# First output projection of a two-layer encoder: seven block products in place of eight, prepared during the attention heads

## The chip, the cores and the metric

One core of one Trainium2 chip runs the whole program. The metric is the device time of one execution in microseconds (us), the median of several runs. The core has five engines with a queue each: PE (TensorE, matrix products into PSUM banks), DVE (VectorE), ACT (ScalarE), POOL (GpSimd) and SP (SyncE, which here issues all the transfers). Each queue runs in its program order; engines wait for one another through semaphores, and while an instruction waits, everything behind it on its engine waits too.

## The reference

The program is an encoder trunk of two layers over 1024 tokens of width 1024, in fp32. Layer 0 is differential attention with 8 heads, layer 1 is latent attention. Cut to what the change touches:

```python
shift, scale, gate = _modulation(c, ada_w[i], ada_b[i])
h = _rmsnorm(x, norm_g[i]) * (1.0 + scale) + shift
# layer 0, _diff_attention:
o = _rmsnorm(o, subln_g) * (1.0 - lambda_init)
o = o.reshape(b, s, DA_WIDTH) * jax.nn.silu(z)
y = o @ w_out                 # (1024, 1024) by (1024, 1024)
...
x = x + gate * y              # gate: one number per output column
```

The change is in `o @ w_out` of layer 0, in where `gate` is applied, and in how `o` and `w_out` come to that product.

## The kernel before

**Products.** An fp32 operand is held as two rounded parts, a high and a low one, and each 128x128 by 128x512 product is three matmuls into one PSUM bank: high by high, high by low, low by high (`mm3`, L186 to L188). To split a 128x512 tile, ACT casts it (the high part) and POOL or DVE subtracts (the low part). In tile names, `wh`, `woh`, `oah`, `oth` are high parts, and `wl`, `wol`, `oal`, `otl` low ones.

**Stages.** From the start of the span: norm, modulation, V and the first K and Q up to about 170 us; heads 0 to 6 of layer 0 up to about 632 us; head 7 up to about 692 us; the first output projection up to 779 us; then layer 1, whose own output projection, at the end of the span, is already made of seven block products (class `Seven`, lines 1827 to 1890 or so).

**A head** (`attn0`) has eight slots: four query tiles by the two halves of differential attention. In a slot PE makes scores, transposes the probabilities and multiplies by V; between these, `FILL0` puts steps of the next head's projections on PE (`acc<-h0h,wh` and so on), whose weights ACT and POOL split (`wl`, L232). At the end of half a head its output goes through the head norm: ACT squares (`osq`), PE sums, POOL does the last step of the reciprocal root (`rq_y`, L173 and L946) and multiplies the output by it (L886) and by the SiLU gate (L931). Hooks run these steps one slot after the other. The last hook (`split`, L889) splits the output on ACT (L894) and POOL (L895) and stores both parts to DRAM (`oS`, L896 and L897).

**The gate.** `gate_steps0` runs one step a slot through heads 0 to 6: loads of the modulation weights and dot products on DVE, five slots for each of eight, then a store to `gateS`.

**Head 7** has no next head to project. From slot 2 on (`Z_LAST`), `extra0` loads outputs and weights of the projection (`pre_plan`), and `PRE0` says how many steps of the projection PE makes in each slot: 12 steps of three matmuls, the heads 0 to 5 of two tiles of 128 tokens (`Pre.step`). `run_tails` ends the head with the calls 8 to 10 of `extra0`.

**The projection** (`out_proj`, L1139) computes four quarters: two groups of 512 tokens by two halves of 512 columns. In a quarter, 8 heads by 4 token tiles make 96 matmuls into four banks named `oacc`; that is 384 in all, 36 of them in head 7. The weights are loaded (`wor`) and split by ACT (L1115) and POOL (L1116, `wol`). The result is multiplied by the broadcast gate on DVE (L1167, `oy<-oacc,gb`, one PSUM and one SBUF input) and added to x (L1168, two SBUF inputs). When a group is complete, its norm runs (`group0`), and steps of the next stage are given out one by one (`side.tick`). The second half of head 7 is finished between the first matmuls of the projection (`tail0`): L933, the sums, `rq_y`, L910, PE's broadcast `rb` (L911), L912, and a split by ACT and DVE (L917).

**Order.** While the table `mk` is filled, POOL's instructions stay in program order (`in_turn`), and ACT's casts and some of DVE's are kept behind the marked ones (`behind`). Elsewhere a scheduler orders each queue when the program is built.

Of the kernel before, what the change touches and what calls it, by code (L numbers as in the profile page):

```python
# [48 lines left out]
PRE0 = (0, 0, 0, 0, 2, 1, 2, 2, 2, 2, 1)  # L49
PRE_N = 6  # L50
PRE1 = (0, 0, 0, 0, 0, 0, 0, 1, 1, 1, 1)
OW0 = (3, 4)
OP0 = (6, 4)
# [31 lines left out]
def trunk(ctx: ExitStack, tc: tile.TileContext, A, out):  # L85
# [49 lines left out]
    oS = dr.tile([NH, 2, 2, P, HF], F32, name="oS")  # L135
    oF = dr.tile([NH, 2, P, HF], F32, name="oF")
    tS = dr.tile([7, 4, P, HF], F32, name="tS")
    sS = dr.tile([4, 2, P, HF], F32, name="sS")
# [741 lines left out]
    def finish(o, y, l, h, half, dst, ap_, dgs):  # L880

        if dst is None:
            b, rb = bcast_rows(ap_, y, "osq", 4)

            def scale():
                in_turn(G.tensor_mul(t3(o), t3(o), rb))  # L886
                hooks.append(split)

            def split():  # L889
                if l == 1:  # L890
                    SP.dma_start(oF[h, half], o)
                    return
                with behind("S"):
                    S.copy(b.bitcast(F32R), o)  # L894
                in_turn(G.tensor_sub(o.bitcast(F32R), o, b))  # L895
# [8 lines left out]
        rb = bank("z" if l else "m", "rb")  # L904
# [8 lines left out]
        if l == 1:  # L913
            return
        hi, lo = dst
        S.copy(hi, o)
        V.tensor_sub(lo, o, f32v(hi))  # L917
# [9 lines left out]
    def subln(o, sq, zz, half, h, dst):  # L927
# [7 lines left out]
        def rest():  # L935
            pt = ssq_at[0] if dst is None and ssq_at else bank("acc" if dst is None else "tr", "ssq")
# [10 lines left out]
            finish(o, y, 0, h, half, dst, a0b if dst is None else None, sq)  # L947

        if dst is None and h < NH - 1:
            hooks.append(rest)  # L950
        else:
            rest()
# [109 lines left out]
    def gate_steps0():  # L1062
# [4 lines left out]
        for j in range(KT):  # L1067
# [3 lines left out]
            for _ in range(5):  # L1071
                yield
# [3 lines left out]
        SP.dma_start(gateS[0].rearrange("(p j) -> p j", p=P), gcol)  # L1076

    gate0 = gate_steps0()
    for h in range(NH - 1):
        attn0(h, lambda i: FILL0[i], lambda i: next(gate0, None))  # L1080
    assert next(gate0, 0) == 0
    def load_ot(dst, src):
        for part_, src_ in zip(dst, src):
            SP.dma_start(f32v(part_), src_)

    class OutW:


        def __init__(self, l, pre, npre, nraw):
            self.l, self.pre, self.npre, self.nraw, self.late, self.nlate = l, pre, npre, nraw, None, 0
            self.gb = pre.tile([P, D], F32, name="gb", tag="gb", bufs=1)
            SP.dma_start(self.gb, gateS[l][None, :].to_broadcast([P, D]))

        def fetch(self, f, h):
            raw = self.pre.tile([P, HF], F32, name="wor", tag="wor", bufs=self.nraw)
            SP.dma_start(raw, A[f"w_out{self.l}"][f, h])
            return raw  # L1100

        def load(self, f, h, spare=False):
            return self.split(self.fetch(f, h), h, spare)

        def split(self, raw, h, spare=False):

            early = h < self.npre
            nb = 2 * self.npre if early else self.nlate
            wpool, tag = (self.pre if early else self.late), "wo"
            if spare:  # L1110
                wpool, tag, nb = wst, "whl", 6
            hi = wpool.tile([P, HF], F32R, name="woh", tag=tag, bufs=nb)
            lo = wpool.tile([P, HF], F32R, name="wol", tag=tag, bufs=nb)
            with behind("S"):
                S.copy(hi, raw)  # L1115
            in_turn(G.tensor_sub(lo, raw, f32v(hi)))  # L1116
            return hi, lo

    def mm_o(acc, OT, W, h, gi, i, n=slice(0, HF)):
        oh, ol = OT[h][gi]  # L1120
        c_ = slice(i * P, (i + 1) * P)
        mm3(acc[:, n], oh[:, c_], ol[:, c_], W[h][0][:, n], W[h][1][:, n], h == 0, h == NH - 1)

    class Pre:


        def __init__(self, OT, W0):
            self.OT, self.W0, self.accs, self.at = OT, W0, [], 0

        def step(self):  # L1130
            if not self.accs:
                self.accs += [bank("acc", "oacc") for _ in range(2)]
                ssq_at.append(self.accs[1])
            i, h = divmod(self.at, PRE_N)
            mm_o(self.accs[i], self.OT, self.W0, h, 0, i)
            self.at += 1
            self.n = self.at // 2

    def out_proj(OT, ow, W0, pre, wpool, xpool, nlate, nx, xsrc, tile_done, group_done):  # L1139

        nonlocal turn
        ow.late, ow.nlate = wpool, nlate

        for gi in range(2):
            fulls = []
            for i in range(4):
                full = xpool.tile([P, D], F32, name="xfull", tag="xfull", bufs=nx)
                SP.dma_start(full, xsrc[gi * 4 + i])
                fulls.append(full)
# [1036 lines left out]
```

## Time and profile before

| what | us |
|---|---|
| median of 3 runs | 1426.74 (1424.81 to 1427.36) |
| the profiled execution | 1425.08 |
| its span, first to last instruction | 1423.3 |
| around the span in that execution | 1.78 |
| PE busy | 1387.4, 97% of the span |
| DVE, ACT, POOL busy | 935.2, 730.0, 658.4 |
| mean granted TensorE clock | 0.996 of full speed |

The profile is of one execution. An engine's busy time is the union of its instructions; matmuls overlap in the records, so a matmul that is listed with 0.39 us starts only about 0.23 us after the one before it, and PE's pace is read from starts. "Idle before <-releaser" gives how long an engine stood still and what ended it. A row of the trace by line gives minimum, median and maximum of one instruction in ns.

### The profile page before, as it was taken

The page shows a single profiled execution, that of the slowest core. Times are in us where ns is not written, and L with a number is a line of the kernel's source. Part 1 is how long each engine was busy: PE and PEld are TensorE (multiplying, and loading weights), DVE is VectorE, ACT ScalarE, POOL GpSimd, SP SyncE. Part 2 cuts the span into 40 slices and gives each one's busy share as a digit, 9 for nine tenths or more (in the row PEclk, how much of TensorE's full clock was granted, in tenths as well). Part 3 has the DMA queues.
Part 4 walks back from the last instruction along what each step waited for, and adds up shares of the span by engine and source line. Part 5 has one row for each costly group of instructions (what it writes and reads, how often), then busy time and mean ns, then how long its engine had stood idle before and what let it go on. Part 6 is the DMA issues. An engine that isn't in the chain of part 4 may idle for free. (4 is left out here: it accounts for less than half of the span.)

```text
span 1423.3 us, 20684 instructions
## 1 busy us (share of the span) xinstructions
PE 1387.4 (97%) x7366; PEld 1155.7 (81%) x7366; DVE 935.2 (66%) x1364; ACT 730.0 (51%) x1299; POOL 658.4 (46%) x520
## 2 busy tenths in 40 slices
PE   9999999999999999998999999999999999999997
PEld 6777788888888887886788777887888888888886
DVE  8665777777777777677435886545666655555685
ACT  5523465656565655566343543335454454545554
POOL 5425254646464646453561324532131165653683
PEclk9999999999999999999999999999999999999999
DMA  9786633333332323236572136398544355566363
GB/s 346 246 244 199 192 88 112 82 112 104 111 112 89 90 90 90 89 101 232 201 221 108 55 111 203 121 301 239 158 124 120 101 166 185 182 212 210 130 252 119
DMA packets 141722, 222.35 MB, mean 156 GB/s; under 512 B 19762, under 2 KB 56754, under 8 KB 141619
## 3 DMA queue, kind: packets, MB, share of 16 engines
q1 hardware_dynamic: 141618, 221.03, 49.2%
q8 instruction: 58, 0.95, 0.3%
q14 instruction: 46, 0.37, 0.1%
HBM read 141.07 MB, written 56.31 MB: 139 GB/s over the span
## 5 line engine op out<-in xcount | busy, mean ns | idle before, releaser
L386 ACT CAST pth<-tr 128x512 fp32r<-128x512 f32 x256 | 150.1, 586 | 288.0 <-PE tr L384 286.2
L401 DVE TENSOR_REDUCE nm<-s 128x1 f32<-128x1024 f32 x192 | 234.0, 1219 | 73.3 <-PE s L848 61.5
L387 DVE TENSOR_TENSOR ptl<-tr,pth 128x512 fp32r<-128x512 f32 x256 | 176.1, 688 | 140.4 <-ACT pth L386 139.8
L232 POOL TENSOR_TENSOR wl<-wraw,wh 128x512 fp32r<-128x512 f32 (+2 forms) x79 | 104.9, 1330 | 211.3 <-ACT wh L231 198.8
L403 ACT ACTIVATE e<-s,nm 128x1024 f32<-128x1024 f32 x128 | 143.6, 1122 | 28.8 <-DVE nm L401 26.6
L384 PE MATMUL tr<-ident,e 128*128 128x128 f32 x1024 | 155.7, 274 | 2.4 <-DVE ptl L387 2.1
L384 PEld LDWEIGHTS tr<-ident,e 128*128 128x128 f32 x1024 | 121.3, 140 | 44.3 <-DVE ptl L387 20.2
L186 PE MATMUL acc<-h0h,wh 128*128 128x512 f32 x360 | 149.8, 416 | 1.1 <-ACT wh L231 0.6
L186 PE MATMUL pv<-pth,vt 128*128 128x256 f32 x512 | 147.8, 289 | 0.0
L187 PE MATMUL pv<-ptl,vt 128*128 128x256 f32 x512 | 145.8, 285 | 0.0
L188 PE MATMUL pv<-pth,vt 128*128 128x256 f32 x512 | 144.6, 282 | 0.0
L188 PE MATMUL acc<-h0h,wl 128*128 128x512 f32 x360 | 143.2, 398 | 0.4 <-POOL wl L232 0.4
L187 PE MATMUL acc<-h0l,wh 128*128 128x512 f32 x360 | 141.9, 394 | 0.0
L187 PEld LDWEIGHTS pv<-ptl,vt 128*128 128x128 f32 x512 | 97.6, 191 | 3.0 <-DVE ptl L387 0.2
L186 PEld LDWEIGHTS pv<-pth,vt 128*128 128x128 f32 x512 | 97.5, 190 | 3.0 <-ACT pth L386 0.4
L188 PEld LDWEIGHTS pv<-pth,vt 128*128 128x128 f32 x512 | 97.5, 191 | 0.1
L328 POOL TENSOR_TENSOR rp_r<-rp_raw,cosT 128x512 f32<-128x512 f32 x38 | 50.0, 1315 | 89.7 <-ACT rp_raw L325 37.9
L333 POOL TENSOR_TENSOR rp_sw<-rp_sw,sinT 128x512 f32<-128x512 f32 x42 | 55.4, 1319 | 70.5 <-DMA rp_sw<-rp_raw 68.0
L848 PE MATMUL s<-ks,qa 128*128 128x512 f32 x256 | 82.3, 403 | 3.8 <-DVE e L856 2.2
L856 DVE SCALAR_TENSOR_TENSOR e<-s,z,e 128x1024 f32<-128x1024 f32 x64 | 82.1, 1283 | 2.0
L848 PE MATMUL s<-ks,qb 128*128 128x512 f32 x256 | 80.7, 396 | 0.0
L188 PEld LDWEIGHTS acc<-h0h,wl 128*128 128x128 f32 x360 | 67.6, 188 | 16.1 <-POOL wl L232 0.8
(505 smaller groups left out, 3406.7 us busy)
## 6 DMA issues: line engine op xcount, KB each, us to landing
ada<-in_ada_ss SPq DMA_DIRECT2D x32, 512.0 KB, 5.6
wraw<-in_w_s SPq DMA_DIRECT2D x64, 256.0 KB, 2.9
vS<-v_hl SPq DMA_DIRECT2D x32, 512.0 KB, 5.9
vt<-vS SPq DMA_DIRECT2D x32, 512.0 KB, 4.3
rp_sw<-rp_raw SPq DMA_DIRECT2D x168, 64.0 KB, 2.0
bc_s<-bc_d SPq DMA_DIRECT2D x34, 256.0 KB, 3.8
wor<-in_w_out SPq DMA_DIRECT2D x32, 256.0 KB, 4.3
wol<-tS SPq DMA_DIRECT2D x28, 256.0 KB, 4.9
```

The lines of the kernel that those rows point to most:

```text
L186: PE.matmul(psum, ah, bh, start=first, stop=False, skip_group_check=skip)
L187: PE.matmul(psum, ah, bl, start=False, stop=False, skip_group_check=skip)
L188: mm3.last = PE.matmul(psum, al, bh, start=False, stop=last, skip_group_check=skip).ins
L232: sub = (V if pair_of else G).tensor_sub(l_[:, :n], raw[:, :n], f32v(h_[:, :n]))
L333: in_turn(G.tensor_mul(sw, sw, sinT[:, cs]))
L384: PE.transpose(tr[:, j, :], p[:, kt * P : (kt + 1) * P], ident)
L386: mk["S"] = S.copy(pth[kh][:, :, dst], tr).ins
L387: mk["V"] = V.tensor_sub(ptl[kh][:, :, dst], tr, f32v(pth[kh][:, :, dst])).ins
L401: mk["V"] = V.reduce_max(nm, s_ps, axis=AX.X, negate=True).ins
L403: mk["S"] = S.activation(e, s_ps, AF.Exp, bias=nm, scale=1.0, accum_out=zs).ins
L848: PE.matmul(s_ps[:, kc * HF : (kc + 1) * HF], src[:, c, ql], KS[h][kc][:, c, :], start=fst, stop=not fst)
L856: combined.append(V.scalar_tensor_tensor(out=e0, in0=e1, scalar=z1[:, 0:1], in1=e0, op0=ALU.mult, op1=ALU.add).ins)
```

## The change

The 1024x1024 by 1024x1024 product becomes seven products of 512x512 blocks by the Strassen-Winograd scheme, each 4 by 4 by 3 = 48 matmuls: 336 in all. The blocks of the left side (`A`) are outputs of a head h and of head h+4 over 512 tokens, or sums of them; the right side (`W`) are blocks of the weights, or sums of them. `n` counts the products, `h` the four pairs of heads.

- **Weights.** The gate is multiplied into the weights instead of the result. `gate_steps0` now takes two slots for a dot product instead of five, then for each h seven slots: two loads in each of two, four POOL products with the broadcast gate, four POOL subtractions, and seven stores to `tS` (two transfers in a slot, the stores a slot or so behind the arithmetic).
- **Outputs.** A head's output is stored unsplit (`oF`, one store, one slot later than the split was). L894, L895 and one of two stores are gone in heads 0 to 7. For h = 0 and 1 the sums of blocks are made on POOL (`combine`, four operations) and stored to `sS` from slots 46 and 54 on; for h = 2 on POOL after head 7 (`k0["pair"]`); for h = 3 on DVE behind the tail of head 7, since they need its last half.
- **Head 7.** Loads start in slot 2, splits of product 0 in slot 3. `PRE0` holds 14 steps: product 0 for two token tiles, then six steps of product 1. The two finished accumulators of product 0 are copied to SBUF (`keep_p1`) and added later on POOL (`add_p1`).
- **The projection.** Products 0 and 1 for the rest, then 2 to 6. Each result is added to the x tiles by DVE (`add0`, one SBUF and one PSUM input); the norm of the first group follows product 4, that of the second product 6.

```diff
-PRE0 = (0, 0, 0, 0, 2, 1, 2, 2, 2, 2, 1)
+PRE0 = (0, 0, 0, 0, 1, 1, 2, 2, 2, 3, 3)
...
             def scale():
                 in_turn(G.tensor_mul(t3(o), t3(o), rb))
-                hooks.append(split)
...
-                with behind("S"):
-                    S.copy(b.bitcast(F32R), o)
-                in_turn(G.tensor_sub(o.bitcast(F32R), o, b))
-                SP.dma_start(oS[h, half, 0], b)
-                SP.dma_start(oS[h, half, 1], o)
+                hooks.append(lambda: hooks.append(store))
+            def store():
+                SP.dma_start(oF[l][h, half], o)
...
+        for h in range(4):
+            b_ = (b11, b12), (b21, b22) = two("ob1"), two("ob2")
...
+                    in_turn(G.tensor_mul(b_[m][f], b_[m][f], gb[f]))
...
+            in_turn(G.tensor_sub(b12, b12, b11))
+            in_turn(G.tensor_sub(t2, b22, b12))
...
+            in_turn(G.tensor_sub(b11, t2, b11))
+            in_turn(G.tensor_sub(b21, b21, t2))
...
+    def combine(a11, a12, a21, a22):
+        in_turn(G.tensor_add(a22, a21, a22))
+        in_turn(G.tensor_sub(a21, a11, a21))
+        yield
+        in_turn(G.tensor_sub(a11, a22, a11))
+        in_turn(G.tensor_sub(a12, a12, a11))
...
+            def g():
+                fin()
+                V.tensor_add(sq, k0["21"], o)
+                V.tensor_sub(k0["21"], k0["11"], k0["21"])
+                V.tensor_sub(k0["11"], sq, k0["11"])
+                V.tensor_sub(k0["12"], k0["12"], k0["11"])
...
-                    y = wpool.tile([P, HF], F32, name="oy", tag="oy", bufs=2)
-                    V.tensor_mul(y, accs[i], ow.gb[:, fs])
-                    V.tensor_add(fulls[i][:, fs], fulls[i][:, fs], y)
...
+    def add_p1(rows, f):
+        for i, t in enumerate(p1s):
+            G.tensor_add(xf[rows + i][:, halves[f]], xf[rows + i][:, halves[f]], t)
+    def add0(tt, acc, f, final=False):
+        V.tensor_add(xf[tt][:, halves[f]], xf[tt][:, halves[f]], acc)
...
+    for h in range(4):
+        for i in range(2, 4):
+            sv0.mm(0, Y[i], h, i, start=True)
+        if h == 0:
+            tail_b = tail0()
+            for _ in combine(*k0["pair"]):
+                pass
...
+    for i in range(2, 4):
+        for h in range(4):
+            sv0.mm(1, Z[i], h, i, start=True)
+            if (i, h) == (3, 1):
+                tail_b()
...
+    for h in range(4):
+        for i in range(4):
+            sv0.mm(2, Y[i], h, i, start=i < 2)
```

Two places of the queues. The first is on POOL around the tail of head 7. Before, behind the split of two weight tiles of the next stage, POOL did the last step of the head norm and then splits of projection weights (`wol`):

```order
L232 TENSOR_TENSOR wl_7755<-wraw_7750,wh_7754 128x512
L232 TENSOR_TENSOR wl_7759<-wraw_7752,wh_7758 128x512
L173 TENSOR_TENSOR rq_y_7172<-sl_w_7166,mhalf_107 128x4
L946 TENSOR_TENSOR rq_y_7172<-rq_y_7172,sl_f_7167 128x4
L1116 TENSOR_TENSOR wol_7246<-wor_7243,woh_7245 128x512
L1116 TENSOR_TENSOR wol_7252<-wor_7249,woh_7251 128x512
```

In the changed kernel, at the same place of POOL's queue, the same step of the norm (L169, L930) is followed by the four sums for h = 2 (`ob`), two additions of a kept accumulator to x (`x0_0`, `x0_1`), and then the first low part of product 2's weights (`wol_7184`); ahead of it stand four splits of product 3's weights:

```order
L1167 TENSOR_TENSOR wol_7274<-wol_7274,woh_7273 128x512
L169 TENSOR_TENSOR rq_y_7227<-sl_w_7221,mhalf_109 128x4
L930 TENSOR_TENSOR rq_y_7227<-rq_y_7227,sl_f_7222 128x4
L1116 TENSOR_TENSOR ob_6967<-ob_6966,ob_6967 128x512
L1373 TENSOR_TENSOR x0_0_7167<-x0_0_7167,p1_7084 128x512
L1117 TENSOR_TENSOR ob_6966<-ob_6964,ob_6966 128x512
L1373 TENSOR_TENSOR x0_1_7168<-x0_1_7168,p1_7086 128x512
L1119 TENSOR_TENSOR ob_6964<-ob_6967,ob_6964 128x512
L1120 TENSOR_TENSOR ob_6965<-ob_6965,ob_6964 128x512
L1167 TENSOR_TENSOR wol_7184<-wol_7184,woh_7183 128x512
```

So between the norm's last step and the first weight that PE's next product needs, six full operations moved in.

The second place is DVE at the same time. Before, once PE had broadcast the norm (`rb`), DVE multiplied the output by it, made the low part, and went on with the finished accumulators:

```order
L910 TENSOR_SCALAR sq7_6608<-ident_89,rq_y_7172 128x128 x4
L912 TENSOR_TENSOR o7_6607<-o7_6607,rb_7175 128x512
L917 TENSOR_TENSOR ot7_l_6606<-o7_6607,ot7_h_6605 128x512
L1167 TENSOR_TENSOR oy_7215<-oacc_6747,gb_6612 128x512
L1167 TENSOR_TENSOR oy_7218<-oacc_6748,gb_6612 128x512
```

In the changed kernel the product with `rb` is followed by the sums for h = 3 (`sq7`, `k21`, `k11`, `k12`), mixed with low parts of products 2 to 4. The row `oal_7335` is the low part of the block of h = 3 for product 2:

```order
L901 TENSOR_TENSOR o7_6664<-o7_6664,rb_7300 128x512
L1332 TENSOR_TENSOR sq7_6665<-k21_6667,o7_6664 128x512
L1376 TENSOR_TENSOR x0_3_7170<-x0_3_7170,oz_7281 128x512
L1333 TENSOR_TENSOR k21_6667<-k11_6666,k21_6667 128x512
L1167 TENSOR_TENSOR oal_7417<-sq7_6665,oah_7416 128x512
L1334 TENSOR_TENSOR k11_6666<-sq7_6665,k11_6666 128x512
L1167 TENSOR_TENSOR oal_7387<-oal_7387,oah_7386 128x512
L1335 TENSOR_TENSOR k12_6668<-k12_6668,k11_6666 128x512
L1167 TENSOR_TENSOR oal_7335<-k11_6666,oah_7334 128x512
```

What stood one operation behind the product with `rb` before now stands eight behind it. On PE, from `rb` on, there are 6 matmuls of product 1 and then product 2, whose 48 matmuls go h by h, twelve to each.

More of the change, by code (lines that the diff above doesn't have):

```diff
@@ L1076, in gate_steps0 @@
         SP.dma_start(gateS[0].rearrange("(p j) -> p j", p=P), gcol)
-    gate0 = gate_steps0()
-    for h in range(NH - 1):
[L1080 to L1113, printed above, removed]
@@ L1889, in trunk, with home_a1 @@
[L1889 to L1900 removed]
+    pw = pool(stO, "pw1", side="right")
+    def home_a1(n):
+        if n in (2, 3, 6):
+            return xt2k("oah"), xt2k("oal")
+        return [op.tile([P, HF], F32R, name="oa" + x_, tag="ab", bufs=16) for x_ in "hl"]
```

490 lines of the change are left out of this document (312 added, 178 removed).

## The prediction

> **What bounds the kernel now.** I read the page's head first, then the busy time by stage, then PE's waits around the projection, then the starts of single instructions. The page:
>
> ```profile
> span 1423.3 us, 20684 instructions
> PE 1387.4 (97%) x7366; PEld 1155.7 (81%) x7366; DVE 935.2 (66%) x1364; ACT 730.0 (51%) x1299; POOL 658.4 (46%) x520
> ```
>
> PE is busy for 97% of the span, so work taken from PE is worth its full time, as long as nothing makes PE wait instead. By stage, the columns being length, then busy time of PE, weight loads, DVE, ACT and POOL, then granted clock, DMA share and GB/s:
>
> ```profile
> 320.00:380.00 60.00, 60.00 (x339) 51.06 (x338) 46.47 (x68) 37.53 (x67) 32.57 (x27) 1.00 0.36 101
> 650.00:660.00 10.00, 7.86 (x44) 5.97 (x44) 7.48 (x13) 6.91 (x13) 4.03 (x3) 1.00 1.02 323
> 670.00:680.00 10.00, 7.45 (x32) 5.48 (x31) 5.46 (x8) 4.76 (x10) 7.97 (x8) 0.83 0.51 176
> 691.46:779.00 87.54, 86.15 (x399) 70.10 (x398) 37.84 (x59) 30.83 (x50) 42.89 (x34) 1.00 0.56 186
> 1372.00:1384.00 12.00, 12.00 (x53) 9.72 (x52) 12.00 (x12) 2.38 (x4) 11.10 (x7) 1.00 0.38 142
> ```
>
> In the heads (first row) PE has no gap and POOL is busy for 54% of the time. Head 7 (second and third) has gaps, transfers that fill the DMA engines, and one stretch at a lower clock. In the projection (fourth) PE stands still for only 1.4 of 87.5 us; POOL is busy for half of it, DVE for less. The last row belongs to the output projection of layer 1, which is made of seven products already: there DVE and POOL are full. What PE waits for between 640 and 790 us:
>
> ```profile
> PE oacc L187 <- POOL wol L1116: 3.9, 4, 2.3
> PE trh L469 <- DVE xfull L458: 1.6, 2, 0.8
> PE rb L911 <- DVE sq L910: 0.9, 1, 0.9
> ```
>
> So around the change PE is the limit, and it is POOL's low parts of weights that come late.
>
> **What goes: 48 matmuls.** PE's pace comes from starts, early and late in the projection:
>
> ```profile
> 712.93 0.39 PE L186 MATMUL oacc<-woh,oth 128*128 128x512 f32 x1
> 714.74 0.39 PE L188 MATMUL oacc<-woh,otl 128*128 128x512 f32 x1
> 777.81 0.40 PE L187 MATMUL oacc<-wol,ot_h 128*128 128x512 f32 x1
> 778.97 0.39 PE L186 MATMUL acc<-h_0h,wh 128*128 128x512 f32 x1
> ```
>
> The first two are eight starts apart: 1.81 / 8 = 0.226 us. The last two are five apart: 1.16 / 5 = 0.232. I take 0.229. 384 matmuls become 336: **-48 x 0.229 = -11.0 us**, if PE stays fed (bounds -10.8 and -11.1).
>
> **Heads 0 to 6: what is added lies beside PE.** POOL gets 16 products, 16 subtractions and 8 sums, and loses the splits of L895 (15 in all):
>
> ```profile
> L895 POOL TENSOR_TENSOR o<-o,bc_s x15: 1265/1288/1302, 220.4 to 689.9; 128x512 fp32r<-128x512 f32 x15
> 426.00 1.29 POOL L232 TENSOR_TENSOR wl<-wraw,wh 128x512 fp32r<-128x512 f32 x1 [2.17 <-ACT wh L231]
> 433.09 1.29 POOL L931 TENSOR_TENSOR o<-o,gz 128x512 f32<-128x512 f32 x1 [5.80 <-ACT o L925]
> 440.89 1.01 POOL L173 TENSOR_TENSOR rq_y<-sl_w,mhalf 128x4 f32<-128x4 f32 x1 [6.51 <-DVE sl_w L944]
> ```
>
> 40 x 1.29 - 14 x 1.29 = 34 us more POOL over some 400 us, in which POOL stands still for about 180 (27.4 of 60 in the first window row). In one slot (a head of 66 us has eight, so 8.2 us each) at most two to three such operations come, 2.6 to 3.9 us, beside 4.5 us of old work (32.57 / 60 x 8.2): it fits, and idle stretches like 5.80 and 6.51 us let a delay run out. DVE loses and gains little: the dot products only come closer together. Transfers: 16 weight loads, 28 stores to `tS`, 8 loads and 8 stores for `sS` of 256 KB are spread over 40 slots where the DMA share is 0.36. I cost it at **0** (bounds -0.5 to +4; the upper end is a rival below).
>
> **Head 7: six matmuls more, and POOL splits both sides.** PE's worst wait of before is here:
>
> ```profile
> 673.87 0.50 PE L187 MATMUL oacc<-wol,oth 128*128 128x512 f32 x1 [2.26 <-POOL wol L1116]
> 675.11 0.80 PE L187 MATMUL oacc<-wol,oth 128*128 128x512 f32 x1 [0.29 <-POOL wol L1116]
> ```
>
> Before, a step needed one POOL split, since outputs came split from DRAM; now it needs two (`both`: A and W), up to six of them between slots 4 and 6, also behind `rq_y` on the same queue. That wait stays. Near the end of the head fewer steps stand between the last transposes and products with V than before, three to eight matmuls less at two places, so DVE's and ACT's copies of the probabilities are covered less. On the other side loads start earlier, with half as many to make (unsplit outputs). The 42 matmuls in place of 36 themselves are only moved forward. I take **+1.2**, about one more split late (bounds: -3 if the 2.26 us and its slow clock go, +4 if they come twice).
>
> **Product 2 waits for its weights.** POOL at the end of head 7 of before, and PE's first projection matmul behind the last product with V:
>
> ```profile
> 691.46 0.39 PE L186 MATMUL oacc<-woh,oth 128*128 128x512 f32 x1
> 693.42 5.05 POOL L1116 TENSOR_TENSOR wol<-wor,woh 128x512 fp32r<-128x512 f32 x4 [2.27 <-ACT woh L1115]
> 701.27 1.01 POOL L173 TENSOR_TENSOR rq_y<-sl_w,mhalf 128x4 f32<-128x4 f32 x1 [0.32 <-DVE sl_w L944]
> 702.36 0.20 POOL L946 TENSOR_TENSOR rq_y<-rq_y,sl_f 128x4 f32<-128x4 f32 x1
> ```
>
> I count from the last product with V. In the changed kernel POOL has four splits first (about 5.1, the second row), whose buffers come free at that moment, then `rq_y` (1.2), then the four sums and two additions, 6 x 1.29 = 7.7, and then `wol_7184`, 1.3: ready at about 15.5. PE has 12 + 18 + 18 + 6 = 54 matmuls until product 2, 12.4 us, and about 1.0 for the small ones of the norm: 13.4. The wait is 2.1; the additions also wait for x, whose loads are issued late behind the weights'. **+2.2** (bounds 0, if the splits start before that moment, and 5, if x comes late). Next behind it on POOL are only further weights of product 2, each needed 12 x 0.229 = 2.7 us after the one before.
>
> **Product 2 waits for its block of h = 3.** DVE's tail of before, and what the sums cost alone and beside POOL in layer 1's projection:
>
> ```profile
> 704.19 0.69 DVE L912 TENSOR_TENSOR o<-o,rb 128x512 f32<-128x512 f32 x1 [0.73 <-PE rb L911]
> 1349.37 0.69 DVE L1957 TENSOR_TENSOR dg<-o1k,o 128x512 f32<-128x512 f32 x1
> 1355.29 7.71 POOL L1868 TENSOR_TENSOR wol<-wol,woh 128x512 fp32r<-128x512 f32 x5
> 1357.55 1.78 DVE L1868 TENSOR_TENSOR oal<-dg,oah 128x512 fp32r<-128x512 f32 x1
> 1361.11 0.67 DVE L1985 TENSOR_TENSOR x<-x,oz 128x512 f32<-128x512 f32 x1
> L1868 DVE TENSOR_TENSOR oal<-oal,oah x11: 679/1191/1774, 1340.9 to 1380.8; 128x512 fp32r<-128x512 f32 x11
> L1868 POOL TENSOR_TENSOR wol<-wol,woh x28: 1277/1302/1824, 1305.3 to 1394.9; 128x512 fp32r<-128x512 f32 x28
> ```
>
> A DVE operation of two SBUF inputs takes 0.69 us while POOL stands still (1349.37) and up to 1.78 while POOL works back to back (1357.55); with one input in PSUM it stays at 0.67 (1361.11). Both engines pay, POOL up to 1.82.
>
> In the changed kernel DVE waits on the way to the tail for POOL's x additions and for ACT's cast of a sum of h = 2 (ready at about 14.6 by the count above), and reaches the product with `rb` at about 18. Eight operations later stands `oal_7335`: 18 + 0.7 + 8 x 0.69 = 24.2 without contention. PE wants it in product 2 behind 36 matmuls: 13.4 + 2.2 + 36 x 0.229 = 23.8. So the wait is 0.4 at least. From `oal_7329` to `oal_7335` eleven operations read two SBUF tiles, and POOL is splitting weights beside them: at the median of 1191 ns they would add 11 x 0.5 = 5.5. But POOL also stands waiting for ACT's casts, so about half of them should meet it: **+3.2** (bounds 0.4 and 12.5, every one of the eleven at 1.78).
>
> The Trainium skill, SBUF — State Buffer, section "SBUF: two separate sides", says that a DVE operation with two SBUF inputs and a GpSimd operation lock one port pair and that the loser stands still for the whole instruction. This trace agrees (1357.55 against 1349.37); taken strictly it speaks for the upper bound and against this change, which moves work onto both engines.
>
> **The clock behind a wait.** In the window from 670 to 680 us the granted clock is 0.83: (1 - 0.83) x 10 = 1.7 us lost, right behind the wait of 2.26. Of two new waits of 2 to 3 us one should do the same: **+1.7** (bounds 0 and 3.4).
>
> The Trainium skill, TensorE: Matmul & The Clock Gate, Part 1, says that only an idle window of about 3.4 us halves the clock. The trace shows it at 2.26 us; by the page's figure this term would be 0.
>
> **The end.** The last group's norm waited for L1167, L1168 and a square over 1024 columns:
>
> ```profile
> L1167 DVE TENSOR_TENSOR oy<-oacc,gb x16: 675/691/692, 706.3 to 780.2; 128x512 f32<-128x512 f32 x16
> L1252 ACT ACTIVATE tjunk<-xfull x8: 1052/1058/1059, 731.5 to 782.7; 128x1024 bf16<-128x1024 f32 x8
> ```
>
> One addition and a square of half the width remain. PE has the next stage's first products beside it and waited only 1.6 us there: **-0.7** (bounds -1.6 and +1).
>
> **The sum.** -11.0 + 0 + 1.2 + 2.2 + 3.2 + 1.7 - 0.7 = **-3.4 us** against the profiled 1425.08, that is 1421.7. That run lies 1.7 below the median of the runs shown, 1426.74; a median for the changed kernel should lie as far above: **1423.3**.
>
> **The rivals.**
>
> *Cover holds.* POOL stands still ahead of the tail, the x loads are early, and the sums meet an idle POOL: no new wait in product 2 and none of its slow clock. -11.0 + 1.2 - 0.7 = -10.5, 1416.2. For it speaks that layer 1's projection, in the same scheme, shows no PE gap (12.00 of 12.00 in the last window row). Against it: there a whole product lies between the norm and product 2; here six matmuls do.
>
> *Every sum meets POOL (slower).* The place is DVE between `oal_7329` and `oal_7335`, the price 1.1 us for each of eleven operations: a wait of 12.5 in place of 3.2, and the sum is +5.9, 1432.6. It turns slower than before once the eleven are lengthened by more than 6.2 us together, 0.56 each; layer 1's median of 1191 is 0.5. For it: POOL has nine weight splits in a row there. Against: `wol` in the projection of before waited for ACT often.
>
> *POOL falls behind in the heads.* An in-order POOL holds a `wl` or a rope behind a product that waits for its weights' load, and PE waits 0.3 us in each of some 30 slots: about +9 in place of 0, 1432. It decides once added work exceeds the 3.7 us that a slot leaves free. Against: the idle stretches above, and loads issued two slots ahead.
>
> **How the numbers follow.** Chances: the forecast's case 0.50, cover holds 0.25, every sum meets POOL 0.12, POOL behind in the heads 0.13. The forecast's own range, with its waits between half and twice, is 1418 to 1428. 0.2% is 2.9 us, about what a measurement of this kernel can tell from no change: faster means below 1423.9. Of the forecast's case I count 0.31 faster, 0.17 within and 0.02 slower; of the contended case 0.04 within and 0.08 slower; of the POOL case 0.01 and 0.12. Together 0.56 faster, 0.22 within, 0.22 slower. The range reaches from a little below the first rival's time to the two slower ones: 1414.5 to 1432.
>
> **What will show it.** In the changed profile: 48 matmuls fewer between head 7 and the next stage; PE unbroken in the heads; PE waits in product 2 for a `wol` and for an `oal` of k11, with the DVE operations of two SBUF inputs before it at 0.69 or above 1.2; a window of clock under 1 behind them. I am wrong on the heads if `wl` shows among PE's waits, on head 7 if its PE idle time differs by more than 3 us, and on the tail if product 2 starts without a gap.

## The result, and the profile after

The changed kernel takes **1430.87 us** (median of 11 runs, 1430.02 to 1433.47) against 1426.93 for the kernel before on the same chip: a ratio of 1.0029, with a 95% interval from 1.0019 to 1.0040. It is slower by 0.3%, where 1423.3 was forecast. Its profiled execution took 1430.70 us, with a span of 1428.9 and a mean granted clock of 0.990 (before: 1425.08, 1423.3 and 0.996).

The head of the page of the changed kernel:

```profile
span 1428.9 us, 20757 instructions
PE 1380.7 (97%) x7318; PEld 1149.6 (80%) x7318; DVE 970.2 (68%) x1383; ACT 737.0 (52%) x1325; POOL 720.0 (50%) x561
```

The 48 matmuls are gone (7366 to 7318), PE is busy 6.7 us less, and the span is 5.6 us longer: PE stands still or runs slowly for longer than it saves. DVE has 35 us more to do, POOL 62. The stages of the changed kernel (length, busy time of PE, weight loads, DVE, ACT and POOL, granted clock, DMA share, GB/s):

```profile
320.00:380.00 60.00, 59.20 (x328) 49.66 (x327) 43.84 (x63) 35.55 (x63) 39.09 (x33) 1.00 0.44 132
690.00:700.00 10.00, 8.20 (x35) 6.60 (x36) 2.11 (x4) 9.13 (x18) 10.00 (x9) 0.83 0.46 165
720.47:726.00 5.53, 5.53 (x20) 4.79 (x21) 3.51 (x5) 1.89 (x4) 2.83 (x3) 0.64 0.01 3
701.83:787.54 85.71, 77.12 (x344) 62.78 (x343) 66.57 (x80) 38.05 (x77) 53.43 (x38) 0.94 0.57 187
```

PE has gaps in this stretch of the heads, where it had none (first row). The last row is the projection from the last product with V on: 54 matmuls fewer than before, worth 12.4 us, but it lasts 85.71 instead of 87.54. PE stands still for 8.6 us in it, and its clock is 0.94 instead of 1.00. What PE waited for between 640 and 800 us:

```profile
PE rb L900 <- DVE x L1376: 6.6, 1, 6.6
PE oy L183 <- POOL wol L1167: 3.6, 3, 2.3
PE tr L380 <- DVE ptl L383: 2.4, 3, 1.7
PE trh L465 <- DVE x L454: 2.0, 2, 1.3
PE pv L182 <- ACT pth L382: 0.7, 1, 0.7
```

The first row is one wait, in front of `rb`, the broadcast of the norm of head 7's last half. What it waits for is not the norm but an addition to x. These are PE's rows around it, and DVE's:

```profile
713.46 0.39 PE L184 MATMUL oz<-woh,oal 128*128 128x512 f32 x1
720.47 1.43 PE L900 MATMUL rb<-sq,ones 128*128 128x128 f32 x5 [6.62 <-DVE x L1376]
```

```profile
708.38 5.03 DVE L899 TENSOR_SCALAR sq<-ident,rq_y 128x128 f32<-128x128 f32 x4 [1.18 <-POOL rq_y L930]
713.33 1.87 DVE L1376 TENSOR_TENSOR x<-x,oy 128x512 f32<-128x512 f32 x3
715.25 1.22 DVE L1167 TENSOR_TENSOR oal<-ob,oah 128x512 fp32r<-128x512 f32 x1
716.40 0.67 DVE L1376 TENSOR_TENSOR x<-x,oy 128x512 f32<-128x512 f32 x1
717.00 2.83 DVE L1167 TENSOR_TENSOR oal<-oal,oah 128x512 fp32r<-128x512 f32 x2
719.75 0.67 DVE L1376 TENSOR_TENSOR x<-x,oz 128x512 f32<-128x512 f32 x1
722.58 0.69 DVE L901 TENSOR_TENSOR o<-o,rb 128x512 f32<-128x512 f32 x1 [1.08 <-PE rb L900]
```

The scaled identities for `rb` (`sq`, first row) are ready at 713.4, just when PE arrives. But `rb` takes a bank of the tag "tr", of which there are two, and both hold a result `oz` of product 1. One comes free when DVE has added it to x (the row at 719.75), and DVE has seven operations ahead of that addition. Three of the seven are low parts, which took 4.05 us together beside a busy POOL; at the 0.69 us of such an operation while POOL stands still they would take 2.1. So by this estimate some 2 of the 6.6 us are DVE's operations taking longer beside POOL, and the rest is what stands ahead in DVE's queue; no run separates the two. From 720.47 to 726 the clock is 0.64 in the mean (third row of the stages), which costs 0.36 x 5.5 = 2.0 us more. It was slow for some 3 us before that, too, but then PE stood still anyway.

The time by stages, worked out from starts of PE's rows: head 0's first scores (`s<-ks`) to head 7's, from there to the last product with V, from there to the first matmul of the next stage, and from there to PE's last matmul. Head 0 varies by 2 us without any edit, so heads 1 to 6 stand beside it. The other kernels of the table are the experiments below.

| kernel | heads 0-6 | heads 1-6 | head 7 | projection | rest |
|---|---|---|---|---|---|
| before | 480.5 | 412.2 | 68.3 | 87.6 | 635.7 |
| changed | 486.5 | 417.6 | 72.1 | 85.8 | 632.9 |
| rb_bank | 485.6 | 416.7 | 73.1 | 84.3 | 634.2 |
| rb_bank_order | 485.7 | 417.0 | 71.6 | 81.7 | 632.6 |
| heads_no_pool | 481.8 | 413.0 | 73.6 | 85.8 | 632.0 |
| heads_memset | 480.5 | 411.7 | 71.1 | 85.5 | 633.3 |
| heads_memset_long | 487.0 | 416.2 | 73.2 | 85.7 | 632.6 |
| heads_dve | 497.8 | 428.4 | 74.1 | 81.5 | 632.9 |
| heads_spread | 492.5 | 423.5 | 73.1 | 81.7 | 631.9 |
| heads_behind_rope | 496.9 | 426.0 | 73.7 | 83.5 | 633.0 |
| p1_early | 490.3 | 419.3 | 73.0 | 83.3 | 634.9 |
| group_wait | 486.9 | 418.0 | 73.1 | 84.9 | 632.3 |
| dots_two_slots | 481.2 | 412.3 | 69.2 | 88.8 | 637.2 |
| spread_and_wait | 492.0 | 423.4 | 71.2 | 82.7 | 633.8 |
| both_parts | 480.8 | 411.9 | 71.9 | 82.0 | 632.2 |
| changed_again | 486.6 | 417.9 | 71.6 | 84.9 | 631.6 |

So of the profiled loss of 5.8 us (PE's last start moves from 1414.6 to 1420.4), the heads are +6.0, head 7 +3.8 (of which six matmuls moved into it are 1.4), the projection -1.8 where -12.4 was to come, the rest -2.8, and 0.6 comes ahead of head 0.

### The profile page after: what moved, and what is told of

Read it like the earlier page. It is cut to its first block, busy times and chain, and to the rows that moved or that the text cites. A ratio compares the mean times of both kernels' runs of the same rounds, so it can differ in the third digit from the quotient of the medians.

```text
span 1428.9 us, 20757 instructions
## 1 busy us (share of the span) xinstructions
PE 1380.7 (97%) x7318; PEld 1149.6 (80%) x7318; DVE 970.2 (68%) x1383; ACT 737.0 (52%) x1325; POOL 720.0 (50%) x561
## 5 line engine op out<-in xcount | busy, mean ns | idle before, releaser
L329 POOL TENSOR_TENSOR rp_sw<-rp_sw,sinT 128x512 f32<-128x512 f32 x42 | 56.8, 1351 | 71.1 <-DMA rp_sw<-rp_raw 71.0
L1167 POOL TENSOR_TENSOR wol<-wol,woh 128x512 fp32r<-128x512 f32 x56 | 82.0, 1489 | 20.5 <-ACT woh L1166 20.5
```

## The experiments

Two theories of the wait at `rb` stood against each other: *bank* (the PSUM bank that an addition on DVE must free) and *port* (the scaled identities are late, since DVE and POOL block one another). Of the heads: *queue* (POOL does its work in order, and 40 more operations make `rp_sw`, the second product of a rope, late, for which DVE waits in order too) and *port* (DVE's own operations are lengthened while POOL reads SBUF). All ratios are to the kernel before on the same chip; the median of before was 1426.1 us for the first four runs, 1428.5 for the next four, 1427.7 for the next three and 1429.0 for the last three. The ratios come from all runs of both kernels, so they can differ a little from the quotient of the medians.

| run | us | ratio to before, 95% |
|---|---|---|
| rb_bank | 1430.56 | 1.0030 (1.0019 to 1.0041) |
| rb_bank_order | 1427.43 | 1.0005 (0.9994 to 1.0016) |
| heads_no_pool | 1426.69 | 1.0005 (0.9993 to 1.0017) |
| heads_memset | 1424.67 | 0.9992 (0.9982 to 1.0003) |
| heads_memset_long | 1430.80 | 1.0015 (1.0002 to 1.0028) |
| heads_dve | 1439.10 | 1.0078 (1.0056 to 1.0100) |
| p1_early | 1430.07 | 1.0017 (1.0002 to 1.0033) |
| dots_two_slots | 1430.78 | 1.0015 (1.0001 to 1.0028) |
| heads_spread | 1434.92 | 1.0039 (1.0025 to 1.0053) |
| group_wait | 1431.93 | 1.0022 (1.0011 to 1.0034) |
| spread_and_wait | 1435.82 | 1.0048 (1.0031 to 1.0064) |
| heads_behind_rope | 1438.52 | 1.0068 (1.0049 to 1.0088) |
| both_parts | 1420.12 | 0.9947 (0.9927 to 0.9966) |
| changed_again | 1430.11 | 1.0013 (1.0002 to 1.0024) |

### rb_bank

```diff
-        rb = bank("z" if l else "tr", "rb", [P, HF])
+        rb = bank("z", "rb", [P, HF]) if l else Y[0]
```

> The broadcast of the norm (rb) goes into one of the four y banks, which stands empty until product 2, instead of the tr bank that DVE must free first; nothing else. Theory 'bank': PE's wait of 6.6 us before rb goes, since the scaled identities for it are ready at about 713.3, when PE arrives at 713.9. But DVE's product with rb keeps its place in the queue, behind the addition to x and three low parts, so product 2, whose first bank is now the one that holds rb, waits until about 721: 4 to 5 us of wait move to product 2 and the slow clock behind it stays; total 1 to 3 us faster than the changed kernel, 1428 to 1430. Rival 'port': the wait was for the scaled identities on DVE (5.03 us beside POOL), not for the bank: rb still starts at about 720 and the time stays at 1431.

PE no longer waits at `rb`, but in front of product 2, for DVE's product with `rb`:

```profile
PE oy L182 <- DVE o L901: 6.1, 1, 6.1
```

The time stays (1.0030 against 1.0029), where 1 to 3 us of gain were expected. *Bank* holds: the wait at `rb` goes as soon as its bank is free. But the work behind it on DVE stands where it stood, and 6.1 of the 6.6 us come back one step later, the case that the expectation gave 4 to 5 for.

### rb_bank_order

As rb_bank, and DVE's order around the tail is changed:

```diff
-    with tc.issue_after(e_last):
-        for _ in sp:
-            pass
+    for _ in range(2):
+        with tc.issue_after(e_last):
+            next(sp), next(sp)
+    with tc.issue_after(k0["k11"]):
+        for _ in sp:
+            pass
...
-        step(sp, h)
+        with tc.issue_after(k0["k11"]):
+            step(sp, h)
```

Here `k0["k11"]` is the sum of L1334; the low parts of A(2,2) and of product 3 are put behind it.

> As rb_bank, and DVE's product with rb and the sums for h = 3 stand ahead of the low parts of A(2,2) and of product 3. Theory 'bank': no wait at rb, product 2 starts at about 717 behind a wait of 1 to 2 us for its first low weight; the 6.6 us and most of 3.4 us of slow clock go, about 1 to 2 us come back: 7 to 9 us faster than the changed kernel, 1422 to 1424. Rival 'port': the sums beside a busy POOL take 1.2 to 1.8 us each, A(2,3) comes 3 to 6 us late and the gain is 2 to 5 us, 1426 to 1429.

DVE's rows behind the scaled identities, and what PE waited for:

```profile
711.45 2.47 DVE L1376 TENSOR_TENSOR x<-x,oy 128x512 f32<-128x512 f32 x4
713.84 0.67 DVE L1376 TENSOR_TENSOR x<-x,oz 128x512 f32<-128x512 f32 x1
714.44 0.67 DVE L901 TENSOR_TENSOR o<-o,oy 128x512 f32<-128x512 f32 x1
```

```profile
PE oy L183 <- POOL wol L1167: 3.6, 3, 2.3
PE trh L465 <- DVE x L454: 3.3, 3, 1.3
PE tr L380 <- DVE ptl L383: 2.4, 3, 1.7
PE oy L182 <- DVE o L901: 1.0, 1, 1.0
...
PE oy L184 <- DVE oal L1167: 0.3, 1, 0.3
```

The product with `rb` comes 8.1 us earlier (722.58 to 714.44, in runs whose last products with V are 1.9 apart, so 6.2), and a wait of 1.0 is left of 6.6. The projection is 81.7 us instead of 85.8, and the median 3.4 us below the changed kernel's 1430.87 (the two ratios to before say the same): inside the range that was expected for the rival, not that of *bank*. The rival's mechanism is there only in part. The sums for h = 3 behind the product with `rb` do take longer beside POOL (1.18, 1.66 and 1.78 us for the second to fourth), but PE waits only 0.3 us for an `oal`. The gain is smaller than *bank* had it because other waits took its place: three for the normalised x (`trh`, 3.3 us) now stand in the projection, 1.3 us more than in the changed kernel, and two for a bank of a later product, 0.9 us. The profiled execution, 1424.35, is the fastest of its twelve.

### heads_no_pool, heads_memset and heads_memset_long

In heads_no_pool the 40 operations of `gate_steps0` on POOL are left out; in heads_memset each is a memset of its tile, in heads_memset_long two memsets and one of half the tile.

```diff
-                    in_turn(G.tensor_mul(b_[m][f], b_[m][f], gb[f]))
+                    in_turn(G.memset(b_[m][f], 0.5))
```

> The changed kernel without POOL's 40 operations in heads 0 to 6 (products of the weights with the gate, their differences, the sums of the outputs for h = 0 and 1); all loads, stores and dot products stay, so the projection gets other data. Theory 'POOL in the heads': these operations cost PE 5 to 6 us there by making rp_sw and small DVE operations late: 5 us faster than the changed kernel, about 1426, head 7 begins at about 633.5 instead of 638.9. Rival 'dot products or transfers': head 7 begins at 637 or later and the time stays within 2 us of the changed kernel, 1429 to 1431.

> The changed kernel, with each of POOL's 40 operations in heads 0 to 6 replaced by a memset of the same 128x512 tile, which reads no SBUF; so the projection gets other data. If 'queue' is the cause (POOL's order holds rp_sw back), the loss shrinks only in proportion to a memset's shorter time. If 'port' is the cause (two-input DVE operations stand still while POOL reads SBUF), DVE's rp_r and sl_f fall back to their durations of before (0.90 and 0.26 us mean, against 1.07 and 0.40 now) whatever a memset takes, and most of 5 us come back: 1426.

> As heads_memset, but each operation is two memsets of the tile and one of its half: 0.53 + 0.53 + 0.27 = 1.33 us, as long on POOL as the 1.30 of the arithmetic, without reading SBUF. Theory 'port': heads 0 to 6 stay as long as in heads_memset and before (480.5 us from the first to the last head's first scores in the trace, against 486.5 in the changed kernel); 1424 to 1426. Rival 'queue': POOL is as late for rp_sw as with the arithmetic, the heads are 485 to 486.5 again; 1429 to 1431.

The group of DVE's rope sum (x28: busy time and mean ns, then idle time before it and what ended it) over 163 to 640 us, for the kernel before, the changed one and heads_no_pool:

```profile
L337 DVE TENSOR_TENSOR rp_r<-rp_r,rp_sw 128x512 f32<-128x512 f32 x28 | 25.1, 898 | 3.6 <-POOL rp_sw L333 3.6
```

```profile
L333 DVE TENSOR_TENSOR rp_r<-rp_r,rp_sw 128x512 f32<-128x512 f32 x28 | 30.0, 1072 | 10.4 <-POOL rp_sw L329 10.2
```

```profile
L333 DVE TENSOR_TENSOR rp_r<-rp_r,rp_sw 128x512 f32<-128x512 f32 x28 | 24.1, 861 | 7.0 <-POOL rp_sw L329 7.0
```

The same of heads_memset, with the memsets' own durations, and of heads_memset_long:

```profile
L333 DVE TENSOR_TENSOR rp_r<-rp_r,rp_sw 128x512 f32<-128x512 f32 x28 | 24.1, 860 | 4.5 <-POOL rp_sw L329 4.5
...
L1083 POOL MEMSET ob<- x16: 520/526/547, 326.6 to 512.7; 128x512 f32 x16
```

```profile
L333 DVE TENSOR_TENSOR rp_r<-rp_r,rp_sw 128x512 f32<-128x512 f32 x28 | 24.2, 864 | 13.7 <-POOL rp_sw L329 13.7
...
L1077 POOL MEMSET ob<- x84: 311/525/545, 329.3 to 542.0; 128x512 f32 x56, 128x256 f32 x28
```

POOL's work is the cause: without it, or with short memsets, heads 1 to 6 take 413.0 and 411.7 us instead of 417.6. The loads, the stores and the dot products all stay in heads_no_pool, so they are not. Which property of POOL's work counts, the two memsets tell apart. Both leave DVE's rope sum at its length (860 and 864 ns against 1072 with the arithmetic). The short one (0.53 us) costs nothing; the long one, which occupies POOL as long as the arithmetic, makes the heads 4.5 us longer, most of the 5.9 that the arithmetic adds to the short memsets. *Queue* holds as the main cause in the heads.

The sum of DVE's waits for `rp_sw` does not measure the loss: heads_no_pool has 7.0 us of them and hardly loses. What counts is where one falls. This is one such place, DVE and PE in the changed kernel and then in heads_memset_long; in heads_memset and heads_no_pool the same rope sum and the same matmul wait for nothing:

```profile
478.99 1.76 DVE L333 TENSOR_TENSOR rp_r<-rp_r,rp_sw 128x512 f32<-128x512 f32 x1 [1.20 <-POOL rp_sw L329]
481.46 0.50 PE L182 MATMUL acc<-h0h,wh 128*128 128x512 f32 x1 [0.87 <-DVE sl_w L926]
```

```profile
481.46 0.69 DVE L333 TENSOR_TENSOR rp_r<-rp_r,rp_sw 128x512 f32<-128x512 f32 x1 [2.18 <-POOL rp_sw L329]
482.87 0.50 PE L182 MATMUL acc<-h0h,wh 128*128 128x512 f32 x1 [0.63 <-DVE sl_w L926]
```

*Port* has a smaller part. Here the changed kernel's rope sum hardly waits, but takes 1.77 us while POOL works on the weights, and PE's transposes behind it wait; below it is the same rope sum in heads_memset_long, where POOL is just as busy with memsets and the transposes do not wait:

```profile
394.88 1.77 DVE L333 TENSOR_TENSOR rp_r<-rp_r,rp_sw 128x512 f32<-128x512 f32 x1 [0.16 <-POOL rp_sw L329]
397.31 0.66 PE L380 MATMUL tr<-ident,e 128*128 128x128 f32 x4 [1.03 <-DVE ptl L383]
```

```profile
397.63 0.69 DVE L333 TENSOR_TENSOR rp_r<-rp_r,rp_sw 128x512 f32<-128x512 f32 x1 [0.29 <-POOL rp_sw L329]
```

Compared matmul by matmul with heads_memset, PE loses 1.2 us here and 0.7 us at 346.5, where a small DVE operation took 1.02 us beside POOL instead of 0.15. These two losses come again in changed_again, rb_bank, rb_bank_order, group_wait and p1_early (1.7 to 1.9 us together) and with neither kind of memset. So of the 5.9 us about 1.9 are *port*'s and about 4 *queue*'s. That the short memset costs nothing, not 40% of the loss, goes further than *queue* had expected: POOL may be occupied for that long without PE losing anything.

### heads_dve

```diff
-            in_turn(G.tensor_sub(t2, b22, b12))
+            V.tensor_sub(t2, b22, b12)
```

All 40 operations of heads 0 to 6 are moved in this way; the base is rb_bank_order.

> rb_bank_order, with the 40 operations of heads 0 to 6 on DVE instead of POOL (the same arithmetic). Theory 'port': DVE holds the pair for 0.69 us in place of POOL's 1.30, but is itself on PE's path and is blocked by POOL's ropes up to 1.8 us each; 40 x 0.7 to 1.2 = 28 to 48 us more on an engine with 13 of 60 us free: PE loses as much as now or more, 1426 to 1434. Rival 'queue': POOL's lateness was the cause, DVE has the room: 4 to 6 us faster than rb_bank_order, 1421 to 1424.

PE's waits over 163 to 640 us:

```profile
PE tr L380 <- DVE ptl L383: 6.4, 6, 3.1
PE s L844 <- DVE e L852: 6.2, 6, 1.9
```

Both kinds of wait are for DVE. The heads grow by 12 us against rb_bank_order, and the run is slower than the range expected: put in this way, the work doesn't fit on DVE either.

### heads_spread and heads_behind_rope

Both have rb_bank_order as base and put POOL's 40 operations in other places: one at a time where POOL waits in a rope, or in pairs behind a rope's subtractions (`stack_k`, `stack_q`).

```diff
+        while spare:
+            fill_pool()
         next(gate0, None)
...
         r_ = eng.tensor_mul(r, raw, cosT[:, cs])
         if eng is G:
             in_turn(r_)
+            fill_pool()
```

> rb_bank_order, with the same 40 POOL operations of heads 0 to 6 put one at a time where POOL waits anyway: behind the first product of a rope (its swapped half is still on its way) and ahead of a rope's two subtractions (ACT still casts); what is left over goes to the slot's end as before. Theory 'queue': POOL's order holds rp_sw back by up to 2.6 us where two operations stand ahead of it; heads 0 to 6 shrink from 485.7 to 481 to 483.5 us, 2 to 4 us faster than rb_bank_order. Rival 'port': DVE still meets POOL's SBUF reads as often, and the heads stay at 485 to 486.5.

> rb_bank_order, with each pair of the 40 POOL operations directly behind a rope's two subtractions, where the next rope's rp_sw is furthest away; what no rope takes goes to the slot's end. Theory 'queue, by its place': none of the pairs stands just ahead of rp_sw any more, DVE's waits for rp_sw fall from 10.2 to 4 to 6 us, heads 0 to 6 from 485.7 to 481 to 484 us, 2 to 4 us faster than rb_bank_order. Rival 'queue, by its sum': some 52 us of POOL more delay something of the rope wherever they stand, and the heads stay within 1.5 us of 485.7 or grow.

Both are slower. In heads_spread heads 2 and 4 come back to 68.4 and 68.0 us (69.3 and 69.9 in the changed kernel), but heads 3 and 5 take 72.1 and 76.0, most of it one event each. The larger one, PE first and then POOL:

```profile
498.10 1.12 PE L389 MATMUL tr<-ident,e 128*128 128x128 f32 x4 [3.11 <-DVE ptl L392]
```

```profile
489.10 1.29 POOL L1103 TENSOR_TENSOR ob<-ob,ot 128x512 f32<-128x512 f32 x1
494.14 1.28 POOL L336 TENSOR_TENSOR rp_sw<-rp_sw,sinT 128x512 f32<-128x512 f32 x1 [3.76 <-DMA rp_sw<-rp_raw]
```

POOL stands idle here: the swapped half of the rope lands late, DVE waits for `rp_sw` in order, and the probabilities behind it wait too. In heads_behind_rope the waits for `rp_sw` are longest:

```profile
DVE rp_r L339 <- POOL rp_sw L335: 16.2, 9, 4.6
```

The theory that the place just ahead of `rp_sw` was what hurt falls; of the places tried, the original one is the least bad. Why the transfer was late at 490 us isn't settled; SP had issued a load and two weight stores just behind it, and the stores of the moved work come at other times too.

### p1_early, group_wait and spread_and_wait

```diff
-PRE0 = (0, 0, 0, 0, 1, 1, 2, 2, 2, 3, 3)
+PRE0 = (0, 0, 0, 0, 2, 1, 2, 3, 2, 2, 2)
```

> rb_bank_order with PRE0 = (0,0,0,0,2,1,2,3,2,2,2): product 0's eight steps end one slot earlier, so the two copies of its accumulators on ACT, which product 1's first matmul waits for, stand ahead of the last casts of the probabilities. If the copies are what empties PE at the end of head 7 (gaps of 1.7, 0.7 and 0.3 us and 3 us of slow clock), 2 to 4 us go: 1423 to 1425. If the gaps are only moved to earlier slots, where low parts of both sides are late, the time stays within 1 us of rb_bank_order's 1427.4.

The second case came, though not within its 1 us: head 7 takes 73.0 us instead of 71.6, and PE waits for a `wol` there more often instead. Its heads 0 to 6 are longer by 4.6 us with the same code, and its profiled execution, 1436.52, is the slowest of its twelve, so its time as a whole says little.

```diff
-G_WAIT = 3
+G_WAIT = 5
```

> rb_bank_order, with the first transposes of the first group's norm two steps later in product 5 (G_WAIT 5 instead of 3). If PE's waits for the normalised x (0.6, 1.3 and 1.3 us) and the slow clock behind them are only a matter of when the transposes stand in PE's queue, they go: 2 to 4 us faster than rb_bank_order. If the norm chain is later than two steps (4 us), nothing or less than 1 us is gained; and the transposes that are pushed behind product 6 may cost 1 us there.

PE's waits between 700 and 800 us:

```profile
PE trh L465 <- DVE h L474: 3.4, 2, 2.5
PE oy L182 <- DVE x L1376: 2.0, 1, 2.0
```

The waits for the normalised x are gone, and others of the same size stand in their place: later transposes wait for DVE's conversion of the earlier ones, and a bank waits for an addition. The projection is longer than rb_bank_order's (84.9 against 81.7). Moving the transposes in PE's queue doesn't take the waits away; it only changes for which of DVE's results PE waits. How much they cost varies: spread_and_wait below has the same edit and waits of the same size there, but its clock stays at full speed in the projection, where group_wait's was halved for 6.8 us, and its projection takes 82.7 us.

> heads_spread and group_wait together, with rb's own bank and order: three of the four losses taken away, head 7 left as it is. The gains are in different stages and should add up: about 1428 - 2 to 4 - 2 to 4, 4 to 8 us faster than rb_bank_order and 3 to 7 us faster than before, ratio to before 0.995 to 0.998.

It shows no gains but the loss of heads_spread again (heads 492.0 us, against 492.5) and a projection of 82.7: 1.0048.

### dots_two_slots

```diff
-            for _ in range(5):
+            for _ in range(2):
```

in the kernel before.

> The kernel before, with the gate's dot products two slots apart instead of five; nothing else. If the bunched dot products on DVE and their 512 KB loads cost PE something in heads 0 to 2, 1 to 2 us slower than before, 1427.5; if not, within 0.7 us of before, 1426.

Its heads 1 to 6 take 412.3 us (before: 412.2): the bunched dot products cost nothing there. Its time is 0.15% above before all the same, with an interval that just excludes 1; where that comes from is open.

### both_parts and changed_again

rb_bank_order and heads_memset in one kernel.

> rb_bank_order together with heads_memset: rb's own bank and order, and a memset in place of each of the 40 operations (so the projection gets other data). If the heads' POOL time and the bank of rb are the two causes of the loss, the gains add: heads at 480.5 us and the projection at 81.7, together 9 to 10 us faster than the changed kernel, 1420 to 1422, and about 5 us faster than before. If another cause takes their place, less than 7 us.

> The changed kernel unaltered, beside the other two: 1430 to 1433, 0.2 to 0.4% above before.

The gains add: 1420.12 against 1430.11 on the same chip, 10.0 us, with heads at 480.8 and the projection at 82.0. The ratio to before is 0.9947 (0.9927 to 0.9966). So two causes account for the loss: POOL's work in the heads, and the bank of `rb` with DVE's order behind it. The unaltered changed kernel is 0.13% above before here, less than the 0.2 to 0.4% expected; its interval overlaps that of the first result (1.0019 to 1.0040). This isn't a version to use, as it leaves out the sums. Of the kernels that compute everything, rb_bank_order is the best with the seven products, and it equals the kernel before (1.0005).

## Why the prediction was wrong

By its own steps, against the profiled executions:

- **48 matmuls, -11.0.** Right: they are gone, and PE's pace between waits is what it was.
- **Heads 0 to 6, 0 (bounds -0.5 to +4).** This is the step that failed by most: +6.0, which alone turns the forecast's -3.4 into +2.6, slower than before. "it fits, and idle stretches like 5.80 and 6.51 us let a delay run out" counted POOL's free time in a slot, and PE indeed never waits for POOL there, so the sign that was to show an error, `wl` among PE's waits, did not come either. But DVE waits for POOL's `rp_sw` in the middle of its own queue, with work for PE behind it (1.20 us at 478.99 above, and 0.87 of PE's time). The two memset runs show that POOL's occupied time is most of it, about 4 us, and the places above that DVE's longer operations beside POOL are about 1.9. The third rival, "POOL falls behind in the heads", came nearest, priced at +9 and given 0.13; but it saw PE lose 0.3 us in each of some 30 slots, and the loss sits in a handful of places of 0.3 to 1.2 us. Its point of decision was wrong: added work costs before it fills a slot, as soon as it delays an operation in the middle of a chain over three engines.
- **Head 7, +1.2 (bounds -3 to +4).** The mechanism was right and its size too small: +3.8, less 1.4 for six matmuls that moved, is +2.4. The waits that were named are there: 2.3 for a `wol` as before, and at the end of the head

```profile
690.79 0.66 PE L380 MATMUL tr<-ident,e 128*128 128x128 f32 x4 [1.68 <-DVE ptl L383]
692.12 0.39 PE L182 MATMUL pv<-pth,vt 128*128 128x256 f32 x1 [0.68 <-ACT pth L382]
692.84 0.66 PE L380 MATMUL tr<-ident,e 128*128 128x128 f32 x4 [0.34 <-DVE ptl L383]
```

  with a clock of 0.83 behind them. What would cure them stays open (p1_early did not).
- **Product 2's waits and their slow clock, +2.2 + 3.2 + 1.7 = 7.1.** The total was near by luck; the place and the cause were wrong. PE stopped one step earlier, at `rb`: 6.6 us, and about 2.0 of clock, 8.6 in all. PE came to `rb` when the prediction's count has it there (13.4 less six matmuls is 12.0 us behind the last product with V; the trace shows 12.1), but the prediction asked only when its inputs come; that its PSUM bank had to be freed by DVE, behind low parts and additions, was not looked at. Once PE had waited there, product 2 started without a gap, the prediction's own sign of being wrong on the tail. rb_bank shows the bank as the cause, and rb_bank_order what remains when the wait is gone: 1.0 before product 2, 0.3 for an `oal`, so the +3.2 for the block of h = 3 was too much even then. The ground for the clock's term was thin, too: it took the slow clock to follow a wait of 2.26 us, but in the changed kernel a wait of 2.28 us, for a `wol` at 680.59, left the clock at 1.00.
- **The end, -0.7.** The rest of the program is 2.8 us shorter, but 2.0 us of waits for the normalised x moved into the projection, at a clock of 0.83 for 10 us, 1.7 more. The net is about +0.9, near the upper bound.
- **DVE beside POOL.** It was priced for operations of two SBUF inputs alone. In the changed kernel the scaled identities, with one tensor input, took 5.03 us for four (row at 708.38 above) where the kernel before shows 0.68 for three:

```profile
702.59 0.68 DVE L910 TENSOR_SCALAR sq<-ident,rq_y 128x128 f32<-128x128 f32 x3 [1.40 <-POOL rq_y L946]
```

  POOL worked back to back beside them, 1.29 us at a time. The Trainium skill, SBUF — State Buffer, section "SBUF: two separate sides", says that a DVE operation in a two-port mode, too, excludes a GpSimd operation for a whole instruction. The trace agrees if these are such operations: 1.26 us for each. It hardly set the time at `rb`: DVE's first low part behind it, at 715.25, had to wait for ACT's cast of a sum of h = 2 anyway, which ended at 715.22. The low parts behind that were lengthened too, and those did count (the estimate of 2 us above).

The rival "every sum meets POOL" did not decide, "cover holds" did not come true either, and the range ended at 1432, with 1430.87 inside it: the sign was wrong.

## What to carry to other kernels

Work put on an engine with free time is not free if that engine serves a short step in the middle of a chain whose next engine waits in order; look for who waits for it, not for its share of busy time. When a matmul is moved behind others, ask of its PSUM bank who frees it and what stands ahead of that on the freeing engine's queue; moving the bank alone only moves the wait, if the work behind it keeps its place. Before eight products become seven, price what prepares them: here the added POOL work in the heads, and one bank with the order of DVE's queue behind it, cost 10 us, nearly all of the 11 that 48 matmuls are worth.

## What the runs showed of the hardware

- A memset of 128x512 fp32 on POOL takes 0.53 us where a product or difference takes 1.30, and while it runs, DVE's sum of two SBUF tiles is not lengthened (0.69 us at 397.63 in heads_memset_long, with memsets on POOL throughout, against 1.77 us beside the arithmetic at 394.88 in the changed kernel; 864 against 1072 ns in the mean).
- A DVE operation on 128x128 with one tensor input took 1.26 us beside a POOL that worked back to back, and 0.23 in the kernel before, where POOL stood still.
- The granted clock fell to 0.83 over 10 us behind waits of 1.7, 0.7 and 0.3 us with matmuls between them, not only behind one wait of 2.3. The Trainium skill, TensorE: Matmul & The Clock Gate, Part 1, speaks of one idle window of about 3.4 us; these traces show less to be enough. Nor does a wait of one length always do it: 2.26 us at 673.87 in the kernel before was followed by a slow clock, 2.28 us at 680.59 in the changed kernel was not.
